# Five places for the low halves of the weights, a negated half made from the high half, and a convolution without padding

## The chip, the core and the metric

The kernel runs on one core of one Trainium2 chip. TensorE does the matmuls; VectorE, ScalarE and GpSimd prepare operands and take results out of PSUM; the queues of SyncE (SP) and GpSimd (POOL) issue the transfers from HBM. The metric is the device time of one launch in microseconds, as the median of the runs shown.

## The reference

Two layers, each of three sublayers with a residual: a SwiGLU feed-forward block (FFN), a mixing sublayer, and another FFN. Sequence 512, model width 1024, all in float32.

```
for l in range(DEPTH):
    h = swiglu_ffn(rmsnorm(x, ffn1_pre_g[l]), ffn1_w_gu[l], ffn1_w_down[l])
    x = x + 0.5 * rmsnorm(h, ffn1_post_g[l])
    h = mixing_sublayer(rmsnorm(x, mix_pre_g[l]), w_in[l], ...)
    x = x + rmsnorm(h, mix_post_g[l])
    h = swiglu_ffn(rmsnorm(x, ffn2_pre_g[l]), ffn2_w_gu[l], ffn2_w_down[l])
    x = x + 0.5 * rmsnorm(h, ffn2_post_g[l])
...
def mixing_sublayer(h, ...):
    z = h @ w_in
    uv, pz, qz, kz, vz, qi, ki, wi, cz, gz = jnp.split(z, ...)
    branches = (gmlp_mixer(uv, ...), pool_mixer(pz, ...), sparse_attention(qz, kz, vz, qi, ki, wi, rel_bias),
                conv_mixer(cz, ...))
    gates = jax.nn.sigmoid(gz.reshape(B, S, N_BRANCH, D_MODEL))
    y = gates[:, :, 0] * (branches[0] @ w_branch[0])
    for n in range(1, N_BRANCH):
        y = y + gates[:, :, n] * (branches[n] @ w_branch[n])
    return y @ w_out
...
def conv_mixer(ab, dw, db, ln_g, ln_b):
    a, gt = jnp.split(ab, 2, axis=-1)
    h = a * jax.nn.sigmoid(gt)
    h = lax.conv_general_dilated(h, dw[:, None, :], window_strides=(1,), padding=[(CONV_K - 1, 0)], ...) + db
    return jax.nn.silu(layernorm(h, ln_g, ln_b))
```

The convolution is causal, depthwise, of 31 taps over 256 channels.

## The kernel before

Everything lies transposed: features on the 128 partitions, the 512 positions along the row. A product of float32 matrices is made of three products in the faster `float32r` type: each operand is split into a high half (rounded) and a low half (the rest), and high x high, high x low and low x high are summed in PSUM. For one tile of 128 output features and 1024 input features that is 24 matmuls of 512 columns (`mm3s`, line 253). They go in this order: for the first seven blocks of inputs high and low half of the weights in turn (so the low half is first needed by the second matmul), then the seven with the low half of x, then the last block's three.

The weights come as tiles of 128x1024 (512 KB) through `weights` (lines 180 to 203). SP loads the tile into `raw` (two places in SBUF). ScalarE makes the high half `wH` from it (line 197; four places). The low half `wL` (four places) is made in one of two ways:

- in the FFNs, VectorE subtracts: `wL = raw - wH` (line 202);
- for tiles called with `far=True`, ScalarE writes the negated high half into `wL` as a rounded, negated copy of `raw` (line 199), and POOL issues a second transfer of the same weights from HBM that is added to it on arrival (line 200). All of the mixing sublayer's columns of `w_in` after the first six, its `w_branch` and the first half of its `w_out` tiles go this way, and the tiles that open a sublayer.

A place of `wH` or `wL` comes free when TensorE has read the tile in it for the last time. The last reader of a low half is the matmul before the last one of its tile, that of a high half the last.

The mixing sublayer (`Mix.rest`) works through 50 columns of `w_in`; the last 32 are the gates (`Mix.gates`). A gate column takes its 24 matmuls, VectorE scales the result (`th`, line 756), ScalarE takes its tanh (line 757), then six matmuls with a `w_branch` tile follow, and VectorE multiplies the two (line 766, or 764 on a branch's first visit). One `w_branch` tile serves four columns and holds its place of `wH` and `wL` all that time, so the columns turn over in the other three. Beside it generators run that are stepped between columns (`pump`): attention with its top-k, the pooling, the gated MLP and the convolution (`conv`), which on VectorE is one multiply-add over 512 positions for each tap and each half of the channels (line 865). The padded input of the convolution (`hp`, tag "cv") has 30 zeros in front, written by POOL (line 699).

The order of the instructions on each engine is fixed when the program is built, by a scheduler that places what its own estimate holds ready. On an engine nothing overtakes: an instruction that waits holds all behind it. Temporaries ("t") have twelve places; in the trace names carry no buffer numbers.

Of the kernel before, what the change touches and what calls it, by code (L numbers as in the profile page):

```python
# [11 lines left out]
F32 = mybir.dt.float32  # L12
F32R = mybir.dt.float32r
I32 = mybir.dt.int32
AF = mybir.ActivationFunctionType
ALU = mybir.AluOpType
AX = mybir.AxisListType

P = 128
N = 512  # L20
# [9 lines left out]
CONV_K = 31  # L30
# [12 lines left out]
V_PS, V_CB, V_LG, V_LB, V_DW = 48, 50, 52, 54, 56  # L43
# [6 lines left out]
class Builder:  # L50
# [17 lines left out]
        return self.sb.tile(shape, dt, name=f"{tag}_{self.n}", tag=tag, bufs=bufs)  # L68

    def tmp(self, dt=F32, w=N):  # L70
        return self.t([P, w], dt, "t", 12)

    def ring(self, dt=F32R):
        return self.t([P, N], dt, "h", 20)
# [105 lines left out]
    def weights(self, src, n, ring=False, raw=None, far=False):  # L180

        nc = self.nc
        raw = raw or self.t([P, 1024], F32, "raw", 2)
        nc.sync.dma_start(raw[:, :n], src)
        if ring:
            hs, ls = [], []
            for i in range(2):
                h, lo = self.ring(), self.ring()
                r = raw[:, i * N:(i + 1) * N]
                nc.scalar.activation(h, r, AF.Copy)  # L190
                nc.gpsimd.tensor_tensor(lo, r, h.bitcast(F32), op=ALU.subtract)
                hs.append(h)
                ls.append(lo)
            return hs, ls
        h = self.t([P, 1024], F32R, "wH", 4)
        lo = self.t([P, 1024], F32R, "wL", 4)
        self.pin(nc.scalar.activation(h[:, :n], raw[:, :n], AF.Copy))  # L197
        if far:
            self.pin(nc.scalar.activation(lo[:, :n], raw[:, :n], AF.Copy, scale=-1.0))  # L199
            nc.gpsimd.dma_start(lo[:, :n], src, accum_op=ALU.add)  # L200
            return h, lo
        self.pin(nc.vector.tensor_tensor(lo[:, :n], raw[:, :n], h.bitcast(F32)[:, :n], op=ALU.subtract))  # L202
        return h, lo
# [362 lines left out]
class Mix:  # L566
# [84 lines left out]
    def rest(self):  # L651
        b, nc, l = self.b, self.b.nc, self.l

        z = self.norm(T_KI)
        kih, kil = b.ring(), b.ring()
        nc.scalar.activation(kih[0:96], z[0:96], AF.Copy)
        nc.scalar.activation(kih[96:128], z[0:32], AF.Copy)
        khf = kih.bitcast(F32)
        nc.vector.tensor_tensor(kil[0:96], z[0:96], khf[0:96], op=ALU.subtract)
        nc.vector.tensor_tensor(kil[96:128], z[0:32], khf[0:32], op=ALU.subtract)  # L660
        pw = b.pt("at")
        for c in range(4):
            nc.tensor.transpose(pw[:, c * 32:(c + 1) * 32], z[96:128, c * P:(c + 1) * P], b.ident[96:128, 96:128])
        self.wi = b.t([P, 4, 4], F32, "wi", 1)
        nc.scalar.activation(self.wi, pw[:, :P].rearrange("p (c k) -> p c k", k=32)[:, :, 0:4], AF.Copy, scale=0.5)
        self.ki = (kih, kil)
        self.qi = b.split(self.norm(T_QI))
        self.q = [b.split(self.norm(T_Q + j, scale=0.125)) for j in range(2)]
        self.k = [b.split(self.norm(T_K + j)) for j in range(2)]
        sc, zv = {}, []  # L670
        for j, i in enumerate((3, 2)):
            sc[i] = self.scores(i)
            zv.append(self.norm(T_V + j))
        sc[1] = self.scores(1)
        zp = [self.norm(T_P)]
        self.vv = []
        for cp in range(2):
            pv = b.pt("at")
            for c in range(2):
                for j in range(2):  # L680
                    nc.tensor.transpose(pv[:, c * 256 + j * P:c * 256 + (j + 1) * P],
                                        zv[j][:, (2 * cp + c) * P:(2 * cp + c + 1) * P], b.ident)
            h, lo = b.t([P, N], F32R, "av", 4), b.t([P, N], F32R, "av", 4)
            b.split(pv, h, lo)
            self.vv.append((h, lo))
        self.busy = False
        attn = [self.attention(i, sc.get(i)) for i in range(4)]
        self.b2 = [(b.ring(), b.ring()) for _ in range(2)]
        b.bg += attn
        pool = [self.pool(zp + [self.norm(T_P + 1)])]  # L690
        b.bg[:0] = pool

        self.hpad = []
        for j in range(2):
            zg = self.norm(T_CZ + 2 + j)
            nc.scalar.activation(zg, zg, AF.Tanh, scale=0.5)
            za = self.norm(T_CZ + j, scale=0.5)
            hp = b.t([P, N + CONV_K - 1], F32, "cv", 2)
            nc.gpsimd.memset(hp[:, 0:CONV_K - 1], 0.0)
            nc.vector.scalar_tensor_tensor(hp[:, CONV_K - 1:], zg, 1.0, za, op0=ALU.add, op1=ALU.mult)  # L700
            self.hpad.append(hp)
        conv = [self.conv()]
        b.bg[:0] = conv
        zv = [self.norm(T_UV + 2 + j) for j in range(2)]
        u = []
        for j in range(2):
            z = self.norm(T_UV + j)
            nc.scalar.activation(z, z, AF.Gelu_apprx_tanh)
            u.append(z)
        gmlp = [self.gmlp(zv, u)]  # L710
        b.bg[:0] = gmlp
        self.y = [None] * KD
        self.ym = []
        b.finish(pool)
        self.gates(1, self.b1, 5000)
        b.finish(gmlp)
        self.gates(0, self.b0, 5000)
        b.finish(conv)
        self.gates(3, self.b3, 5000)
        b.finish(attn)  # L720
        self.gates(2, self.b2, 5000)
        self.o = [None] * KD
        self.sq = b.tmp()
        for d0 in range(0, KD - TAIL, 2):
            ds = range(d0, d0 + 2)
            w = [b.weights(b.a["w_out"][l, d], 1024, far=True) for d in ds]
            p = [b.cyc() for d in ds]
            b.gemms(p, w, self.ym)
            for i, d in enumerate(ds):
                self.o[d] = b.t([P, N], F32, "y", 8)  # L730
                nc.scalar.activation(self.o[d], p[i], AF.Copy)
                b.sq_add(self.sq, self.o[d], FULL, d == 0)
# [121 lines left out]
    def conv(self):  # L854
        b, nc, l = self.b, self.b.nc, self.l
        acc = []
        ca = b.t([P, 2 * N], F32, "ca", 1)
        for j in range(2):
            a = ca[:, j * N:(j + 1) * N]
            hp = self.hpad[j]  # L860
            dw = lambda t: b.v(l, V_DW + t * 2 + j)
            nc.vector.tensor_scalar(a, hp[:, 0:N], dw(0), b.v(l, V_CB + j), op0=ALU.mult, op1=ALU.add)
            yield 450
            for t in range(1, CONV_K):
                nc.vector.scalar_tensor_tensor(a, hp[:, t:t + N], dw(t), a, op0=ALU.mult, op1=ALU.add)  # L865
                if t % 2 == 0:
                    yield 1360
            acc.append(a)
        both = b.tmp()
        nc.gpsimd.tensor_tensor(both, acc[0], acc[1], op=ALU.add)  # L870
        yield 0, 1
        ps = b.compact([both], FULL)
        mu = b.s8(4)
        nc.vector.tensor_scalar(mu, ps, 1.0 / C, None, op0=ALU.mult)
        dg = b.diag(mu, FULL, 1.0)
        yield 500, 1
        pb = b.spread(dg, FULL)
        sq = []
        for j in range(2):
            nc.vector.tensor_tensor(acc[j], acc[j], pb, op=ALU.subtract)  # L880
            q = b.tmp()
            nc.scalar.activation(q, acc[j], AF.Square)
            sq.append(q)
        nc.gpsimd.tensor_tensor(sq[0], sq[0], sq[1], op=ALU.add)
        yield 1200, 1
        ps = b.compact([sq[0]], FULL)
        ms, r = b.s8(4), b.s8(4)
        nc.vector.tensor_scalar(ms, ps, 1.0 / C, EPS, op0=ALU.mult, op1=ALU.add)
        b.rsqrt(r, ms)
        dg = b.diag(r, FULL)  # L890
        yield 1500, 1
        pb = b.spread(dg, FULL)
        self.b3 = []
        for j in range(2):
            nc.vector.tensor_tensor(acc[j], acc[j], pb, op=ALU.mult)
            nc.vector.tensor_scalar(acc[j], acc[j], self.ln2[:, j:j + 1], self.ln2[:, 2 + j:3 + j],
                                    op0=ALU.mult, op1=ALU.add)
            th = b.tmp()
            nc.scalar.activation(th, acc[j], AF.Tanh)
            nc.vector.scalar_tensor_tensor(th, th, 1.0, acc[j], op0=ALU.add, op1=ALU.mult)  # L900
            self.b3.append(b.split(th))
            yield 2300
# [165 lines left out]
```

## Time and profile before

| | |
|---|---|
| median of three runs | 2319.39 us (2319.12 to 2322.17) |
| the profiled execution | 2320.38 us, of it 2318.7 us span |
| TensorE busy | 2279.7 us, 98% of the span |
| VectorE busy | 1192.4 us, 51% |
| ScalarE busy | 924.5 us, 40% |
| GpSimd busy | 249.8 us, 11% |
| mean granted TensorE clock | 0.996 |

The mixing sublayers lie at about 385 to 760 us and 1530 to 1905 us, the FFNs around them. TensorE is at work nearly all the time, so what a change is worth is what it takes from, or adds to, the few stretches in which TensorE stands still. Of its 39 us of idle time some 9 lie ahead of the first products and some 14 behind the last; the rest is in the mixing sublayers and at the seams.

### The profile page before, as it was taken

The numbers are of one execution on the slowest core, as the hardware profiler recorded it, in microseconds if no ns is written. First come the engines' busy times: TensorE is split into PE (matmuls) and PEld (weight loads), VectorE is DVE, ScalarE is ACT, GpSimd is POOL, SyncE is SP. The second block draws the span as 40 slices with busy tenths as digits, with TensorE's granted clock in tenths as the row PEclk, the third lists the DMA queues.
The fourth block names the chain that finished last, engine by engine and source line by source line (L and its number), as shares of the span: only waits on it lengthen the run. The fifth ranks groups of instructions, "written<-read, shape, count | busy, mean of one in ns | idle before, by whom it ended". The sixth has DMA issues, their size and how long they took to land.

```text
span 2318.7 us, 28250 instructions
## 1 busy us (share of the span) xinstructions
PE 2279.7 (98%) x11158; PEld 1907.0 (82%) x11158; DVE 1192.4 (51%) x2144; ACT 924.5 (40%) x1350; POOL 249.8 (11%) x291
## 2 busy tenths in 40 slices
PE   8999999999999999999999999999999999999997
PEld 6888889777788988888888888897778889888886
DVE  5333337799433552434473334478984337424345
ACT  4232225564554532222342222355545545322221
POOL 0000002211331200000100000023123212000001
PEclk9999999999999999999999999999999999999998
DMA  5333323867778433233343333247677774332322
GB/s 170 92 107 92 108 90 94 187 148 169 176 167 182 119 100 98 93 101 95 94 113 95 110 92 100 91 122 162 148 180 178 174 164 110 100 93 93 105 88 68
DMA packets 82557, 282.27 MB, mean 122 GB/s; under 512 B 9428, under 2 KB 13176, under 8 KB 82424
## 3 DMA queue, kind: packets, MB, share of 16 engines
q1 hardware_dynamic: 64136, 213.87, 29.2%
q0 software_dynamic: 18288, 66.59, 16.7%
q8 instruction: 87, 1.43, 0.2%
q14 instruction: 46, 0.38, 0.0%
HBM read 278.32 MB, written 2.10 MB: 121 GB/s over the span
## 4 chain that ended last, share of the span: by engine, by line
PE 88%; DVE 6%; DMA 2%; ACT 2%; issue 2%; POOL 0%; SPq 0%; POOLq 0%; DVEq 0%; ACTq 0%
PE mm L253 51%; PE at L253 31%; DVE ca L865 2%; PE mm L287 2%; PE at L287 2%; DMA wL<-in_w_in_dram 1%; DMA raw<-in_w_in_dram 1%; ACT wH L197 1%; PE st L330 1%; PE st L314 1%; ACT wL L199 1%; DMA wL<-in_ffn_w_gu_dram 0%; ACT xH L408 0%; DVE sc L935 0%; DVE m L934 0%
## 5 line engine op out<-in xcount | busy, mean ns | idle before, releaser
L197 ACT ACTIVATE wH<-raw 128x1024 fp32r<-128x1024 f32 (+1 forms) x394 | 407.4, 1037 | 831.4 <-issue 562.6
L253 PE MATMUL mm<-xH,wH 128*128 128x512 f32 x1344 | 530.8, 396 | 1.5 <-DVE t L756 1.5
L253 PE MATMUL mm<-xH,wL 128*128 128x512 f32 x1344 | 525.7, 392 | 5.3 <-DMA wL<-in_w_in_dram 5.3
L202 DVE TENSOR_TENSOR wL<-raw,wH 128x1024 fp32r<-128x1024 f32 (+1 forms) x272 | 324.2, 1194 | 248.5 <-ACT wH L197 248.4
L253 PE MATMUL mm<-h,wH 128*128 128x512 f32 (+1 forms) x1496 | 409.2, 354 | 0.3 <-DVE t L756 0.3
L253 PE MATMUL mm<-xL,wH 128*128 128x512 f32 x1344 | 358.9, 389 | 0.0
L253 PEld LDWEIGHTS mm<-xH,wL 128*128 128x128 f32 x1344 | 253.6, 189 | 60.2 <-DMA wL<-in_w_in_dram 7.6
L253 PEld LDWEIGHTS mm<-xH,wH 128*128 128x128 f32 x1344 | 253.5, 189 | 58.5 <-issue 4.2
L253 PEld LDWEIGHTS mm<-h,wH 128*128 128x128 f32 x1496 | 263.8, 188 | 41.7 <-DVE t L756 0.5
L253 PEld LDWEIGHTS mm<-xL,wH 128*128 128x128 f32 x1344 | 252.3, 188 | 52.4
L253 PE MATMUL at<-xH,wH 128*128 128x512 f32 x704 | 277.8, 396 | 8.1 <-ACT xH L223 7.3
L253 PE MATMUL at<-xH,wL 128*128 128x512 f32 x704 | 274.5, 392 | 0.0
L253 PE MATMUL mm<-h,wL 128*128 128x512 f32 (+1 forms) x748 | 252.4, 352 | 0.0
L253 PE MATMUL at<-h,wH 128*128 128x512 f32 (+1 forms) x776 | 219.6, 366 | 0.0
L199 ACT ACTIVATE wL<-raw 128x1024 fp32r<-128x1024 f32 x122 | 128.6, 1054 | 179.5 <-PE mm L253 151.0
L253 PE MATMUL at<-xL,wH 128*128 128x512 f32 x704 | 187.8, 389 | 0.0
L253 PEld LDWEIGHTS at<-xH,wH 128*128 128x128 f32 x704 | 133.1, 189 | 38.6 <-ACT xH L223 7.7
L253 PEld LDWEIGHTS at<-h,wH 128*128 128x128 f32 x776 | 140.4, 188 | 24.6
L253 PEld LDWEIGHTS at<-xH,wL 128*128 128x128 f32 x704 | 133.1, 189 | 29.5 <-issue 1.4
L253 PEld LDWEIGHTS mm<-h,wL 128*128 128x128 f32 x748 | 140.4, 188 | 20.3
L253 PEld LDWEIGHTS at<-xL,wH 128*128 128x128 f32 x704 | 132.2, 188 | 27.5
L253 PE MATMUL at<-h,wL 128*128 128x512 f32 (+1 forms) x388 | 136.5, 366 | 0.0
(212 smaller groups left out, 2260.7 us busy)
## 6 DMA issues: line engine op xcount, KB each, us to landing
raw<-in_ffn_w_gu_dram SPq DMA_DIRECT2D x173, 512.0 KB, 3.6
raw<-in_w_in_dram SPq DMA_DIRECT2D x98, 512.0 KB, 6.5
wL<-in_w_in_dram POOLq DMA_DIRECT2D x94, 512.0 KB, 7.1
raw<-in_ffn_w_down_dram SPq DMA_DIRECT2D x64, 448.0 KB, 3.3
raw<-in_ffn_w_down_dram SPq DMA_DIRECT2D x32, 512.0 KB, 3.5
raw<-in_w_branch_dram SPq DMA_DIRECT2D x16, 512.0 KB, 5.3
wL<-in_w_branch_dram POOLq DMA_DIRECT2D x16, 512.0 KB, 7.0
raw<-in_w_out_dram SPq DMA_DIRECT2D x16, 512.0 KB, 6.3
```

Source lines behind the costliest of these rows:

```text
L197: self.pin(nc.scalar.activation(h[:, :n], raw[:, :n], AF.Copy))
L199: self.pin(nc.scalar.activation(lo[:, :n], raw[:, :n], AF.Copy, scale=-1.0))
L202: self.pin(nc.vector.tensor_tensor(lo[:, :n], raw[:, :n], h.bitcast(F32)[:, :n], op=ALU.subtract))
L253: self.nc.tensor.matmul(out, w[a], m[b], start=(first and i == 0), stop=(last and i == 3 * n - 1))
L287: self.nc.tensor.matmul(out, w[a], m[b], start=(count[j] == 1), stop=(count[j] == 3 * KD))
L314: self.nc.tensor.matmul(ps[:, c - c0:c - c0 + 1], s[:, c * P:(c + 1) * P], self.ones[:, 0:1], start=(i == 0), stop=(i == len(tiles) - 1))
L330: self.nc.tensor.matmul(ps[:, s], self.ones, dg[:, s], start=True, stop=True)
L865: nc.vector.scalar_tensor_tensor(a, hp[:, t:t + N], dw(t), a, op0=ALU.mult, op1=ALU.add)
```

## The change

Four things are changed.

1. `wL` has five places instead of four; `wH` keeps four. The room comes from the temporaries, which go from twelve places to eleven.
2. The negated half of a `far` tile is read from `wH` instead of `raw` (line 199): ScalarE now has to write `wH` first.
3. The convolution's input has no padding: `hp` is 512 wide, its two zero-fills on POOL are gone.
4. The taps run from the last to the first, and tap `s` covers the 512 - s positions that it reaches.

```diff
     def tmp(self, dt=F32, w=N):
-        return self.t([P, w], dt, "t", 12)
+        return self.t([P, w], dt, "t", 11)
...
         h = self.t([P, 1024], F32R, "wH", 4)
-        lo = self.t([P, 1024], F32R, "wL", 4)
+        lo = self.t([P, 1024], F32R, "wL", 5)
         self.pin(nc.scalar.activation(h[:, :n], raw[:, :n], AF.Copy))
         if far:
-            self.pin(nc.scalar.activation(lo[:, :n], raw[:, :n], AF.Copy, scale=-1.0))
+            self.pin(nc.scalar.activation(lo[:, :n], h.bitcast(F32)[:, :n], AF.Copy, scale=-1.0))
             nc.gpsimd.dma_start(lo[:, :n], src, accum_op=ALU.add)
             return h, lo
...
-            hp = b.t([P, N + CONV_K - 1], F32, "cv", 2)
-            nc.gpsimd.memset(hp[:, 0:CONV_K - 1], 0.0)
-            nc.vector.scalar_tensor_tensor(hp[:, CONV_K - 1:], zg, 1.0, za, op0=ALU.add, op1=ALU.mult)
+            hp = b.t([P, N], F32, "cv", 2)
+            nc.vector.scalar_tensor_tensor(hp, zg, 1.0, za, op0=ALU.add, op1=ALU.mult)
...
-            nc.vector.tensor_scalar(a, hp[:, 0:N], dw(0), b.v(l, V_CB + j), op0=ALU.mult, op1=ALU.add)
+            nc.vector.tensor_scalar(a, hp, dw(CONV_K - 1), b.v(l, V_CB + j), op0=ALU.mult, op1=ALU.add)
             yield 450
-            for t in range(1, CONV_K):
-                nc.vector.scalar_tensor_tensor(a, hp[:, t:t + N], dw(t), a, op0=ALU.mult, op1=ALU.add)
-                if t % 2 == 0:
+            for s in range(1, CONV_K):
+                nc.vector.scalar_tensor_tensor(a[:, s:], hp[:, :N - s], dw(CONV_K - 1 - s), a[:, s:],
+                                               op0=ALU.mult, op1=ALU.add)
+                if s % 2 == 0:
                     yield 1360
```

The order on the engines moves with it. On ScalarE, among the last gate columns of layer 0 (`wL_5836` belongs to the tile first multiplied at 718 us in the trace; `t` with line 757 is the tanh of the column that has just been finished, `h` with line 223 the split of a finished sum), the rows stand so before:

```order
L199 ACTIVATE wL_5836<-raw_5833 128x1024
L197 ACTIVATE wH_5835<-raw_5833 128x1024
L757 ACTIVATE t_5762<-t_5762 128x512
L223 ACTIVATE h_5774<-y_4150 128x512
L199 ACTIVATE wL_5884<-raw_5881 128x1024
L197 ACTIVATE wH_5883<-raw_5881 128x1024
L757 ACTIVATE t_5810<-t_5810 128x512
```

and so after the change:

```order
L197 ACTIVATE wH_5833<-raw_5831 128x1024
L756 ACTIVATE t_5760<-t_5760 128x512
L199 ACTIVATE wL_5834<-wH_5833 128x1024
L223 ACTIVATE h_5772<-y_4148 128x512
L197 ACTIVATE wH_5881<-raw_5879 128x1024
L756 ACTIVATE t_5808<-t_5808 128x512
L199 ACTIVATE wL_5882<-wH_5881 128x1024
```

The negated half stood first in each round and now stands third, behind the high half and the tanh.

On ScalarE, in the first round of gates of layer 0 (`wL_4253` is first multiplied at 530 us; `s` and line 957 to 959 are the softmax of the attention, line 220 the splits of other branches), before:

```order
L959 ACTIVATE t_4097<-t_4097,s_789_4101 128x256
L199 ACTIVATE wL_4253<-raw_4250 128x1024
L197 ACTIVATE wH_4252<-raw_4250 128x1024
L757 ACTIVATE t_4140<-t_4140 128x512
L199 ACTIVATE wL_4316<-raw_4313 128x1024
L220 ACTIVATE y_4173<-t_4053 128x512
L757 ACTIVATE t_4209<-t_4209 128x512
L197 ACTIVATE wH_4315<-raw_4313 128x1024
```

and after:

```order
L959 ACTIVATE t_4095<-t_4095,s_789_4099 128x256
L197 ACTIVATE wH_4250<-raw_4248 128x1024
L199 ACTIVATE wL_4251<-wH_4250 128x1024
L756 ACTIVATE t_4138<-t_4138 128x512
L197 ACTIVATE wH_4313<-raw_4311 128x1024
L220 ACTIVATE y_4171<-t_4051 128x512
L756 ACTIVATE t_4207<-t_4207 128x512
L220 ACTIVATE t_4227<-at_4222 128x512
L199 ACTIVATE wL_4314<-wH_4313 128x1024
```

Here the first negated half moves behind its high half, with nothing else between; the second one moves from the fifth row to the ninth, behind a tanh and two splits.

On VectorE, at the attention's split that TensorE waits for at 482 us (`t_3756`, line 221), before:

```order
L865 SCALAR_TENSOR_TENSOR ca_3767<-cv_3716,vec,ca_3767 128x512
L865 SCALAR_TENSOR_TENSOR ca_3767<-cv_3568,vec,ca_3767 128x512
L865 SCALAR_TENSOR_TENSOR ca_3767<-cv_3716,vec,ca_3767 128x512
L865 SCALAR_TENSOR_TENSOR ca_3767<-cv_3568,vec,ca_3767 128x512
L221 TENSOR_TENSOR t_3756<-at_3752,t_3755 128x256
```

and after:

```order
L864 SCALAR_TENSOR_TENSOR ca_3765<-cv_3715,vec,ca_3765 128x511
L864 SCALAR_TENSOR_TENSOR ca_3765<-cv_3568,vec,ca_3765 128x504
L864 SCALAR_TENSOR_TENSOR ca_3765<-cv_3715,vec,ca_3765 128x510
L864 SCALAR_TENSOR_TENSOR ca_3765<-cv_3568,vec,ca_3765 128x503
L864 SCALAR_TENSOR_TENSOR ca_3765<-cv_3715,vec,ca_3765 128x509
L221 TENSOR_TENSOR t_3754<-at_3750,t_3753 128x256
```

The same taps stand ahead of the split; they are a little shorter.

## Rows read from the trace of the kernel before

**Rows 1.** Stretches of the two mixing sublayers: us, busy by engine, clock, DMA share, GB/s.

```profile
400.00:760.00 360.00, 352.60 (x1648) 286.09 (x1648) 232.77 (x501) 196.78 (x299) 89.78 (x104) 0.99 0.74 168
...
1540.00:1900.00 360.00, 353.37 (x1699) 288.49 (x1698) 239.81 (x512) 199.90 (x305) 91.11 (x103) 1.00 0.73 167
```

**Rows 2.** Timeline of TensorE, matmuls that waited: start, us, [idle before <-releaser].

```profile
482.53 0.41 PE L253 MATMUL at<-t,av 128*128 128x256 f32 x1 [2.37 <-DVE t L221]
...
530.16 0.50 PE L253 MATMUL mm<-xH,wL 128*128 128x512 f32 x1 [3.09 <-DMA wL<-in_w_in_dram]
...
570.96 0.50 PE L253 MATMUL mm<-xH,wL 128*128 128x512 f32 x1 [0.54 <-DMA wL<-in_w_in_dram]
...
1673.21 0.50 PE L253 MATMUL mm<-xH,wL 128*128 128x512 f32 x1 [0.23 <-DMA wL<-in_w_in_dram]
...
1682.08 0.55 PE L969 MATMUL at<-ident,t 128*128 128x128 f32 x3 [1.87 <-ACT t L959]
...
1684.81 0.50 PE L253 MATMUL mm<-xH,wL 128*128 128x512 f32 x1 [0.57 <-DMA wL<-in_w_in_dram]
...
1695.33 0.50 PE L253 MATMUL mm<-xH,wH 128*128 128x512 f32 x1 [1.52 <-DVE t L756]
```

**Rows 3.** Waits, all engines: who waited for whom: us in total, times, longest.

```profile
ACT wL L199 <- PE mm L253: 151.0, 55, 5.2
...
PE mm L253 <- DMA wL<-in_w_in_dram: 5.3, 5, 3.1
```

**Rows 4.** Timeline of ScalarE in one round of the last gates.

```profile
710.05 1.06 ACT L199 ACTIVATE wL<-raw 128x1024 fp32r<-128x1024 f32 x1 [2.24 <-PE mm L253]
711.02 1.04 ACT L197 ACTIVATE wH<-raw 128x1024 fp32r<-128x1024 f32 x1
711.96 0.61 ACT L757 ACTIVATE t<-t 128x512 f32<-128x512 f32 x1
```

**Rows 5.** POOL's part of that round: its timeline, then the tile's time to landing.

```profile
711.41 0.86 POOL L200 DMA_DIRECT2D wL<-in_w_in_dram  x1 [6.04 <-ACT wL L199]
...
DMA to landing us min/median/max: 6.9/6.9/6.9
```

**Rows 6.** Timeline of TensorE, first uses of the tile: high half, low half.

```profile
718.35 0.40 PE L253 MATMUL mm<-xH,wH 128*128 128x512 f32 x1
718.58 0.39 PE L253 MATMUL mm<-xH,wL 128*128 128x512 f32 x1
```

**Rows 7.** Timeline of VectorE: the scaling ahead of a tanh, in three rounds.

```profile
562.55 0.69 DVE L756 TENSOR_TENSOR t<-mm,rb__553_3031 128x512 f32<-128x512 f32 x1
...
710.28 0.69 DVE L756 TENSOR_TENSOR t<-mm,rb__553_3031 128x512 f32<-128x512 f32 x1 [1.74 <-PE mm L253]
...
1711.11 0.68 DVE L756 TENSOR_TENSOR t<-mm,rb__2307_12256 128x512 f32<-128x512 f32 x1
```

**Rows 8.** Timeline of ScalarE at 561 us.

```profile
561.72 1.06 ACT L199 ACTIVATE wL<-raw 128x1024 fp32r<-128x1024 f32 x1 [1.84 <-PE mm L253]
```

**Rows 9.** A tile of w_out: negation, time to landing, first uses of two tiles' low halves.

```profile
737.57 1.06 ACT L199 ACTIVATE wL<-raw 128x1024 fp32r<-128x1024 f32 x1 [2.24 <-PE mm L253]
...
DMA to landing us min/median/max: 6.8/6.8/6.8
...
746.33 0.62 PE L253 MATMUL at<-h,wL 128*128 128x512 f32 x2
```

**Rows 10.** Two rounds of layer 1: ScalarE's negations, TensorE's first use of the first.

```profile
1701.31 1.04 ACT L199 ACTIVATE wL<-raw 128x1024 fp32r<-128x1024 f32 x1
...
1707.74 1.06 ACT L199 ACTIVATE wL<-raw 128x1024 fp32r<-128x1024 f32 x1 [2.23 <-PE mm L253]
...
1709.45 0.50 PE L253 MATMUL mm<-xH,wL 128*128 128x512 f32 x1
```

**Rows 11.** The taps of the convolution, line 865: times, ns min/median/max.

```profile
L865 DVE SCALAR_TENSOR_TENSOR ca<-cv,vec,ca x120: 723/743/2241, 467.1 to 1704.8; 128x512 f32<-128x512 f32 x120
```

**Rows 12.** The stretch around a long wait; the last three figures are clock, DMA, GB/s.

```profile
527.00:535.00 8.00, 4.91 (x15) 3.86 (x15) 8.00 (x19) 5.22 (x7) 0.07 (x2) 0.79 0.91 225
```

## The prediction

> **What bounds the kernel now.** I read the stretches first. In the two windows that hold the mixing sublayers TensorE is busy 352.6 of 360 us and 353.4 of 360 [rows 1], and the 14 us missing there are nearly all that a change inside these sublayers can win back. So the question is which TensorE waits there are, and what ends each. The timeline of TensorE gives them [rows 2]: some end with the arrival of a low half of weights (530, 571, 1673, 1685 us), some with VectorE or a softmax (482, 1682, 1695 us). All waits for low halves of `w_in` sum to 5.3 us, five times [rows 3]. Then I followed one round of the last gate columns, to see how near the others are to waiting. The negation starts at 710.05, the moment TensorE frees the place [rows 4]; the transfer is issued at 711.41 and lands 6.9 us later [rows 5], at 718.3; TensorE first reads the tile at 718.58 [rows 6]. So 0.3 us are to spare. Such rounds do not show in any list of waits, yet anything that makes the negation later than 0.3 us stops TensorE there.
>
> **The fifth place.** ScalarE's negation has waited 151 us in total for TensorE to free a place of `wL` [rows 3]; with five places that wait goes. But the negation now reads `wH`, which keeps four places, and a high half's place comes free one matmul after the low half's: 0.23 us by two starts in a row [rows 6]. The wait moves one instruction ahead, to the high half. Gain 0, and 0.23 us are lost.
>
> The Trainium skill, Perfetto Trace Analysis, section Optimization Strategy, says that gaps repeating on the engine that should be saturated can mean that there is no SBUF for the next tile, buffer count among the reasons. It speaks for a fifth place; by it the 5.3 us would go, and it is the first rival below. The rows fit its diagnosis, but the place that is short after the change is one that the change does not add.
>
> **The order on ScalarE, the main term.** In a round of the last gates the order was negation, high half, tanh; it becomes high half, tanh, negation. The high half takes 0.97 us from start to start [rows 4]. The tanh needs VectorE's scaling, which ends at 710.28 + 0.69 = 710.97 [rows 7], before the high half would be done; so it runs at once and takes 0.5 to 0.6 us [rows 4]. The negation comes 0.23 + 0.97 + 0.55 = 1.7 us later, and with it everything up to the landing. Of that 0.3 us are covered: TensorE waits 1.4 us. The next column is as tight, but its place is freed before this wait and its use comes after, so the wait covers it: counted once for such a pair. The six places where this decides, by their rows:
>
> - 530 us: TensorE already waits 3.09 us [rows 2]; the order there puts only the high half ahead, so +1.0 [rows 4].
> - 571 us: it already waits 0.54 us [rows 2], so nothing is covered. The negation was at 561.72 [rows 8]; VectorE's scaling ends at 562.55 + 0.69 = 563.24 [rows 7], the tanh at about 563.9, so the negation is 2.1 us late: +2.1.
> - last gates of layer 0: +1.4, as above.
> - `w_out`, layer 0: negated at 737.57, issued 1.36 us later as in [rows 4, 5], landed after 6.8 us at 745.7; its first use is the second of two matmuls from 746.33 [rows 9], so about 0.8 us are to spare, and 1.7 - 0.8 = +0.9.
> - the last gates and `w_out` of layer 1 are built the same: +1.4 and +0.9.
> - layer 1, 1709 and 1716 us: at 1701.31 the negation gets the high half ahead of it. Its landing, after 1.36 and about 6.9 us, is 1709.6, and TensorE reads it at 1709.45 [rows 10], so nothing is to spare: +1.0. The next one was at 1707.74 [rows 10] and will stand behind a tanh whose scaling VectorE finished only at 1711.79 [rows 7]; that would be 4.7 us late. From it go the 1.0 us for which TensorE was just held and what VectorE has gained by then. Bounds 0.5 (VectorE in time: 1.7 - 1.0 - 0.2) and 3.5 us; I take 2.0.
>
> The stretch of 1673 to 1696 us in layer 1 has two waits for low halves and two for VectorE's work [rows 2]. The low halves come later by 1.0 and about 2 us. But where TensorE is held, VectorE's work goes on, and the two waits it caused, 1.87 and 1.52 us [rows 2], shrink by as much. Between 0 (all absorbed) and 3.0 us (nothing) I take 1.5.
>
> Sum: layer 0, 1.0 + 2.1 + 1.4 + 0.9 = 5.4; layer 1, 1.5 + 1.0 + 2.0 + 1.4 + 0.9 = 6.8; together 12.2 us. The remaining rounds of the gates have more than 1.4 us to spare and add tenths at most.
>
> **The raw tile** is now read by one ScalarE instruction instead of two, so SP's next load starts about 1 us sooner. No TensorE wait in the list ends with a raw tile [rows 2]: 0.
>
> **The convolution.** The 30 shortened taps leave out 1 + 2 + ... + 30 = 465 positions for each half of the channels. At 743 ns for 512 positions [rows 11] that is at most 465 x 1.45 ns = 0.7 us for each of two halves, 1.35 us of VectorE a layer. TensorE's wait at 482 us (2.37 us [rows 2]) stands behind taps, but the same number as before, and the few shortened by then save under 0.1 us. Gain 0 to 1.3 us a layer; taken as 0, since it is counted in the two bounds above. The two zero-fills were POOL's alone, of 30 columns: 0.
>
> **One temporary fewer.** No row shows a wait for a temporary's place. Bounds: 0, and the longest wait for a softmax row, 1.87 us [rows 2]. Taken as 0, since the order on VectorE is nearly the same. In the FFNs the low half was always made from the high half, so neither the fifth place nor the order moves anything there: 0.
>
> **The clock.** Around the 3.09 us wait the mean granted clock was 0.79 over 8 us [rows 12]: 3.4 us at the lower of the two levels, 1.2 GHz, which costs 1.7 us of work. That wait stays. Of the new waits, those at 571 and 1716 us (2.7 and 2 us) are nearest to it in length. I leave the clock out of the sum and put it into the range.
>
> **The rivals.**
>
> *The fifth place pays.* If the negation were in fact ready sooner (the high half's place free well before the low half's), the waits for low halves would go: 5.3 us [rows 3], and 1.7 us of clock, 2312.4 us. It ends on the other side, and it decides at the place: if `wH` is free when the low half's fifth place is. Against it: the high half's last reader follows the low half's in every tile, and both have held four. Chance 0.08.
>
> *The delay is mostly covered.* Where VectorE lets the tanh run late in all rounds or TensorE's other waits absorb it, only 530, 571 and the last gates count, about +5: 2324.5. For it: VectorE's waits in both layers [rows 2]. Against it: the last gates of both layers have no such wait. Chance 0.20.
>
> *All hidden.* Transfers land sooner since ScalarE starts them further apart, and nothing moves: 2319. Against it: a delay of 1.7 us stands against a spare of 0.3 us in the last gates. Chance 0.05.
>
> *The clock falls too.* The waits at 571, 1685 and 1716 us each bring the lower level, at 1.7 us: 2331.5 + 5 = 2336.6, and more if what I called absorbed is not. Chance 0.12.
>
> **How the numbers follow.** The profiled execution took 2320.38 us, 1.0 above the median of the runs. 2320.4 + 12.2 = 2332.6; against the median, 2331.6, rounded to 2331.5. This forecast (2326 to 2335) has chance 0.55. The range goes from the covered case with its lower edge (2321) to the clock case (2338); outside lie the first rival, part of the hidden case, and the far end of the clock case, some 0.16. A difference of 0.2% (4.6 us) is about what a measurement of this kernel tells from none. Slower by more: the forecast, the clock case and six tenths of the covered case, 0.55 + 0.12 + 0.12 = 0.79. Within 0.2%: the hidden case and the rest of the covered one, 0.13. Faster: 0.08.
>
> **What the profile after would show.** Right: ScalarE's wait for TensorE stands at line 197, and line 199 waits for it no more; TensorE waits 1 to 2 us for a low half near the ends of both layers' gates and 0.5 to 1 us at `w_out`; the total of its waits for `wL` is near 17 us instead of 5.3; the FFN stretches keep their time. Wrong: TensorE's busy share of the mixing sublayers stays or rises, the last gates show no wait, or a new wait stands at a temporary or at SP's loads.

## The result, and the profile after

| | before | after |
|---|---|---|
| median of the runs, us | 2319.55 | 2338.55 |
| profiled execution: its time, us | 2320.38 | 2340.61 |
| its span, us | 2318.7 | 2338.9 |
| TensorE busy, us | 2279.7 | 2289.6 |
| TensorE idle (span less busy), us | 39.0 | 49.3 |
| mean granted clock of TensorE | 0.996 | 0.993 |

The changed kernel is slower. The medians lie 19.0 us apart; over all runs the ratio is 1.0076, with a 95% interval of 1.0064 to 1.0087, some 18 us. The forecast was 2331.5, in a range of 2321 to 2338: the median lies 0.55 us above its upper edge, while 1.0076 times the 2319.39 us that the forecast started from is 2337.0, inside it. The profiled execution lost 20.2 us: TensorE is idle for 10.3 us more and busy for 9.9 us more, at the same number of matmuls.

The page of the changed kernel, its busy times:

```profile
PE 2289.6 (98%) x11158; PEld 1911.6 (82%) x11158; DVE 1196.1 (51%) x2144; ACT 927.4 (40%) x1350; POOL 246.6 (11%) x287
```

The table of its waits, which answers to [rows 3] (us in total, times, longest):

```profile
PE mm L253 <- DMA wL<-in_w_in_dram: 19.0, 11, 3.9
...
ACT wH L197 <- PE mm L253: 307.8, 89, 8.9
```

and the second of these rows in the kernel before:

```profile
ACT wH L197 <- PE mm L253: 94.3, 24, 8.8
```

TensorE now waits 19.0 us for low halves of `w_in`, not 5.3. ScalarE's wait for TensorE at line 197 has grown from 94.3 to 307.8 us; at line 199, where it was 151.0 us, there is none. The seven longest of TensorE's eleven waits for low halves, from its timeline, as [rows 2]:

```profile
506.38 0.70 PE L253 MATMUL mm<-xH,wL 128*128 128x512 f32 x1 [3.89 <-DMA wL<-in_w_in_dram]
...
573.70 0.50 PE L253 MATMUL mm<-xH,wL 128*128 128x512 f32 x1 [2.14 <-DMA wL<-in_w_in_dram]
...
732.58 0.50 PE L253 MATMUL mm<-xH,wL 128*128 128x512 f32 x1 [1.44 <-DMA wL<-in_w_in_dram]
...
1663.01 0.50 PE L253 MATMUL mm<-xH,wL 128*128 128x512 f32 x1 [2.82 <-DMA wL<-in_w_in_dram]
...
1729.97 0.50 PE L253 MATMUL mm<-xH,wL 128*128 128x512 f32 x1 [3.05 <-DMA wL<-in_w_in_dram]
...
1761.38 0.50 PE L253 MATMUL mm<-xH,wL 128*128 128x512 f32 x1 [1.06 <-DMA wL<-in_w_in_dram]
...
1888.16 0.50 PE L253 MATMUL mm<-xH,wL 128*128 128x512 f32 x1 [2.18 <-DMA wL<-in_w_in_dram]
```

The round of [rows 4 to 6] in the changed kernel: ScalarE, then the issue on POOL, then TensorE's first use of the low half.

```profile
715.60 1.06 ACT L197 ACTIVATE wH<-raw 128x1024 fp32r<-128x1024 f32 x1 [3.19 <-PE mm L253]
716.56 0.61 ACT L756 ACTIVATE t<-t 128x512 f32<-128x512 f32 x1
717.08 1.04 ACT L199 ACTIVATE wL<-wH 128x1024 fp32r<-128x1024 f32 x1
...
718.41 0.86 POOL L200 DMA_DIRECT2D wL<-in_w_in_dram  x1 [6.04 <-ACT wL L199]
...
724.01 0.50 PE L253 MATMUL mm<-xH,wL 128*128 128x512 f32 x1
```

High half, tanh, negation: the negation begins 1.48 us after the high half, which is 0.96 + 0.52 from the three starts. That is the order, and with the 0.23 us of the place the delay, that the prediction gave for this round.

One stretch ahead of the gates holds the longest wait. ScalarE there, after:

```profile
490.12 1.06 ACT L197 ACTIVATE wH<-raw 128x1024 fp32r<-128x1024 f32 x1
...
494.89 0.63 ACT L707 ACTIVATE t<-t 128x512 f32<-128x512 f32 x1 [2.41 <-DVE t L646]
...
498.87 0.51 ACT L959 ACTIVATE t<-t,s 128x256 f32<-128x256 f32 x1 [0.77 <-DVE s L958]
499.29 1.05 ACT L199 ACTIVATE wL<-wH 128x1024 fp32r<-128x1024 f32 x1
```

and before, where the negation came first:

```profile
489.78 1.06 ACT L199 ACTIVATE wL<-raw 128x1024 fp32r<-128x1024 f32 x1 [0.98 <-PE mm L253]
```

Between the high half and the negation made from it now stand the GELU of the gated MLP (line 707), which waits for VectorE, and three steps of a softmax, 9.2 us from start to start. The transfer lands at 506.3 and TensorE waits 3.89 us. The same piece of the order in layer 1, there 8.9 us from start to start, gives the 2.82 us at 1663.

The clock: 8 us windows around the places where it fell (the last three figures are clock, DMA share, GB/s). Before, in the middle of the kernel, only those around 482 and 530 us read 0.79, the second in [rows 12], the first here:

```profile
479.00:487.00 8.00, 5.63 (x20) 0.79 1.01 246
```

After:

```profile
503.00:511.00 8.00, 4.62 (x13) 0.79 0.92 219
571.00:579.00 8.00, 5.86 (x19) 0.79 1.04 256
1571.00:1579.00 8.00, 7.69 (x28) 0.79 0.96 219
1636.00:1644.00 8.00, 5.87 (x20) 0.79 1.00 239
1660.00:1668.00 8.00, 5.18 (x16) 0.79 0.92 215
1885.00:1893.00 8.00, 5.82 (x19) 0.79 1.04 256
```

Six falls to the lower level (1.2 GHz) instead of two. At the 1.7 us that the prediction worked out for one, four more are 6.8 of TensorE's 9.9 us of longer busy time.

### The profile page after: what moved, and what is told of

Same layout as the page of the kernel before. It is cut to its first block, busy times and chain, and to the rows that moved or that the text cites. A ratio compares the mean times of both kernels' runs of the same rounds, so it can differ in the third digit from the quotient of the medians.

```text
span 2338.9 us, 28346 instructions
## 1 busy us (share of the span) xinstructions
PE 2289.6 (98%) x11158; PEld 1911.6 (82%) x11158; DVE 1196.1 (51%) x2144; ACT 927.4 (40%) x1350; POOL 246.6 (11%) x287
## 4 chain that ended last, share of the span: by engine, by line
PE 79%; DVE 7%; issue 7%; DMA 3%; ACT 2%; POOL 1%; POOLq 0%; SPq 0%; DVEq 0%; ACTq 0%
PE mm L253 42%; PE at L253 31%; DMA wL<-in_w_in_dram 2%; PE mm L287 2%; PE at L287 2%; DVE sc L935 1%; DVE m L934 1%; DVE ca L864 1%; POOL wL L200 1%; PE st L330 1%; ACT wH L197 1%; PE st L314 1%; ACT wL L199 0%; ACT xH L408 0%; DVE t L400 0%
## 5 line engine op out<-in xcount | busy, mean ns | idle before, releaser
L199 ACT ACTIVATE wL<-wH 128x1024 fp32r<-128x1024 f32 x127 | 133.2, 1049 | 1.2
```

The lines of the kernel that those rows point to most:

```text
L199: self.pin(nc.scalar.activation(lo[:, :n], h.bitcast(F32)[:, :n], AF.Copy, scale=-1.0))
```

## The experiments

All ratios are against runs of the kernel before on the same chip, with 95% intervals. Theory 1 was the prediction's: the loss comes from the source of the negation, because the place that is short is that of the high half.

**Which part carries the loss.** First the change without its second part:

```
-            self.pin(nc.scalar.activation(lo[:, :n], h.bitcast(F32)[:, :n], AF.Copy, scale=-1.0))
+            self.pin(nc.scalar.activation(lo[:, :n], raw[:, :n], AF.Copy, scale=-1.0))
```

> The changed kernel with one line put back: the negated half is again made from raw (five places for low halves, four for high halves, eleven temporaries and the unpadded convolution stay). Theory 1, the negation's source: it no longer stands behind the high half and the tanh, so the 20 us go and the fifth place is even used; TensorE's waits for low halves fall below the 5.3 us of the kernel before, 2312 to 2318 us. Theory 2, the loss sits in the other parts (one temporary fewer, the convolution, a changed order on VectorE): 2330 to 2338 us, and the waits for low halves stay near 19 us.

Measured: 2444.38 us, ratio 1.0526 (1.0507 to 1.0546). Both theories fell for this run: it is 106 us slower than the full change. Its timeline of ScalarE, and SyncE's queue in the same stretch (three loads from 609.48 on):

```profile
607.45 1.06 ACT L199 ACTIVATE wL<-raw 128x1024 fp32r<-128x1024 f32 x1 [7.58 <-DMA raw<-in_w_in_dram]
608.41 1.04 ACT L197 ACTIVATE wH<-raw 128x1024 fp32r<-128x1024 f32 x1
...
616.21 1.06 ACT L199 ACTIVATE wL<-raw 128x1024 fp32r<-128x1024 f32 x1 [6.24 <-DMA raw<-in_w_in_dram]
...
609.48 17.73 SPq L184 DMA_DIRECT2D raw<-in_w_in_dram  x3
```

The time from issue to landing of the raw tiles there:

```profile
DMA to landing us min/median/max: 6.2/6.4/6.5
```

and the negation's wait for raw tiles in the whole run:

```profile
ACT wL L199 <- DMA raw<-in_w_in_dram: 298.0, 69, 8.0
```

The high half at 608.41 belongs to the tile before the one negated at 607.45. With a free low place the negation runs one tile ahead of the high half, so a tile stays in `raw` from its negation to its high half, some 10 us, and both raw places are taken. The next load goes out only after the high half (609.48), lands 6.4 us later, and ScalarE stands for it until 616.21 with tanh and softmax behind it. So the second part of the change is also what makes a fifth low place bearable with two `raw` places.

Then the second part alone, on the kernel before:

```
-            self.pin(nc.scalar.activation(lo[:, :n], raw[:, :n], AF.Copy, scale=-1.0))
+            self.pin(nc.scalar.activation(lo[:, :n], h.bitcast(F32)[:, :n], AF.Copy, scale=-1.0))
```

> The kernel before with only the source of the negation changed to the high half (four and four places, twelve temporaries, padded convolution). Theory 1: the source alone carries the loss, 2333 to 2340 us, ScalarE's wait for TensorE moves from the negation to the high half, and TensorE's waits for low halves come to 15 to 20 us. Theory 2: 2318 to 2324 us.

Measured: 2334.19 us, ratio 1.0049 (1.0030 to 1.0069); the medians lie 13.4 us apart. From its waits:

```profile
PE mm L253 <- DMA wL<-in_w_in_dram: 18.1, 12, 3.5
...
ACT wH L197 <- PE mm L253: 307.1, 91, 8.9
```

Both waits are within a microsecond of those of the full change. Theory 1 holds: the source of the negation carries most of the loss without any of the other parts.

**Which place is short.** In the changed kernel, the fifth place goes to the high halves:

```
-        h = self.t([P, 1024], F32R, "wH", 4)
-        lo = self.t([P, 1024], F32R, "wL", 5)
+        h = self.t([P, 1024], F32R, "wH", 5)
+        lo = self.t([P, 1024], F32R, "wL", 4)
```

> The changed kernel with the fifth place given to the high halves instead of the low ones (wH 5, wL 4); the negation still reads the high half. Theory 1a, the place that is short is that of the high half: the high half is written a tile early, the negation waits only for its own place as in the kernel before, 2314 to 2322 us, ScalarE's wait for TensorE is back at the negation. Theory 1b, it is the order alone (the negation stands behind the tanh whichever place is free): 2333 to 2340 us.

Measured: 2317.25 us, ratio 0.9984 (0.9974 to 0.9995). From its waits:

```profile
PE mm L253 <- DMA wL<-in_w_in_dram: 3.4, 3, 1.4
```

Its timeline of ScalarE in the round that answers to [rows 4]:

```profile
707.93 1.06 ACT L199 ACTIVATE wL<-wH 128x1024 fp32r<-128x1024 f32 x1 [2.24 <-PE mm L253]
708.90 1.05 ACT L197 ACTIVATE wH<-raw 128x1024 fp32r<-128x1024 f32 x1
709.85 0.61 ACT L756 ACTIVATE t<-t 128x512 f32<-128x512 f32 x1
```

The negation still reads the high half, but that half was written a tile earlier; it waits 2.24 us for its own place, to the hundredth as in [rows 4], and the next high half and the tanh stand behind it. With the right place the loss is gone and a little more. The place and the order move together here: with a high half's place free early, the scheduler also puts the negation ahead of the tanh again, and no run holds one of the two still while the other moves. The Trainium skill, Perfetto Trace Analysis, section Optimization Strategy, says that repeated gaps can point to the buffer count; here they did, but it was a fifth place for the high halves, and not the one for the low halves, that filled them (3.4 us of waits against 19.0 us).

The low halves back at four, all else as changed:

```
-        lo = self.t([P, 1024], F32R, "wL", 5)
+        lo = self.t([P, 1024], F32R, "wL", 4)
```

> The changed kernel with the low halves back at four places; everything else of the change stays (negation from the high half, eleven temporaries, unpadded convolution). The order of instructions on every engine is the same as in the changed kernel. Theory 1, the fifth place is never used, since the negation waits for the high half, whose place comes free last: the same time as the changed kernel, 2335 to 2341 us, TensorE's waits for low halves 17 to 21 us. Rival, the fifth place gives back part of the loss: 2342 us or more without it.

Measured: 2339.43 us, ratio 1.0084 (1.0071 to 1.0098), with this wait:

```profile
PE mm L253 <- DMA wL<-in_w_in_dram: 18.4, 14, 4.5
```

The fifth low place does nothing in the changed kernel: without it the order is the same and so is the time.

Five places for both:

```
-        return self.t([P, w], dt, "t", 11)
+        return self.t([P, w], dt, "t", 9)
-        h = self.t([P, 1024], F32R, "wH", 4)
+        h = self.t([P, 1024], F32R, "wH", 5)
```

> Five places for both halves, paid with two more temporaries (nine instead of eleven); the negation reads the high half. Theory 1a: neither half waits for a place when its turn comes, the transfers go out up to a tile earlier, TensorE's waits for low halves nearly vanish, 2308 to 2316 us. Against it: nine temporaries delay the softmax and the taps on VectorE, waits for VectorE's temporaries appear, 2320 to 2340 us.

Measured: 2319.99 us, ratio 0.9992 (0.9982 to 1.0002): no difference from before. The page has no wait ahead of the matmuls that read low halves (the last figure):

```profile
L253 PE MATMUL mm<-xH,wL 128*128 128x512 f32 x1344 | 525.5, 392 | 0.0
```

The waits for low halves are gone, and nothing is gained: TensorE's waits for VectorE's scaling grew from 1.8 to 3.4 us and for VectorE's low halves (line 221) from 4.7 to 6.8 us. Which of the nine temporaries and the new order did that was not told apart.

**The small parts.** The unpadded convolution alone on the kernel before (the lines of `conv` as in the change), and then with eleven temporaries too:

```
-            hp = b.t([P, N + CONV_K - 1], F32, "cv", 2)
+            hp = b.t([P, N], F32, "cv", 2)
...
-        return self.t([P, w], dt, "t", 12)
+        return self.t([P, w], dt, "t", 11)
```

> The kernel before with the unpadded convolution alone (places four and four, twelve temporaries, negation from raw). Theory of the prediction: 0, with 1.35 us of VectorE less a layer: 2317 to 2322 us. Rival: the part of the loss that the negation alone did not show (19.0 - 13.4 = about 5.6 us) comes from the convolution's new order on VectorE: 2323 to 2328 us.

> The unpadded convolution and eleven temporaries on the kernel before (negation from raw, places four and four). Against the run with the convolution alone it shows the temporary. Prediction: 0, 2317 to 2322 us. Rival: the missing temporary makes a wait on VectorE or ScalarE and costs 2 to 6 us, 2323 to 2328 us.

Measured: 2322.03 us, ratio 1.0010 (1.0001 to 1.0019), and 2322.27 us, ratio 1.0009 (1.0000 to 1.0018). The convolution by itself costs about 2 us, hardly clear of nothing, and the temporary adds nothing that these runs can tell. In the first of the two TensorE's waits for low halves are 6.3 us instead of 5.3 and those for VectorE's scaling 3.0 instead of 1.8, although VectorE is busy for 1.1 us less.

Between the medians the parts alone sum to 13.4 + 2.2 = 15.6 of 19.0 us. The rest, 3.4 us, lies within the interval of the negation's part (7 to 16 us) and was not traced to a part of the change. It is hardly waiting: in the profiled execution with the negation alone, the fastest of its four, TensorE is idle for 47.3 us against 49.3 in the full change, but busy for 2282.8 us against 2289.6, at a mean granted clock of 0.995 against 0.993.

**POOL.** In 26 of the 60 rounds of the gates and `w_out` after them (each issue's start less its negation's), the issue comes 0.8 us or so later than elsewhere, since a gate's addition now stands ahead of it on POOL. The additions go to VectorE:

```
-                e = nc.vector if n == 2 else nc.gpsimd
+                e = nc.vector
```

> The changed kernel with the gates' additions to y (28 of 512 columns on GpSimd, 1.28 us each) moved to VectorE, so that no addition stands ahead of a transfer's issue on GpSimd. In the changed kernel 26 of 60 issues come 0.8 us or more later than the 1.35 us after the negation's start that the others show. If that is a part of the loss, TensorE's waits for low halves fall from 19 to 8 to 13 us, and the time to 2328 to 2334 us. If VectorE's longer rounds (0.65 us more for each column) hold the tanh and so the negation, nothing is won: 2337 us or more.

Measured: 2339.89 us, ratio 1.0086 (1.0073 to 1.0100); nothing is won. The time from issue to landing, 576 to 770 us, of this run:

```profile
DMA to landing us min/median/max: 5.4/6.6/8.5
```

of the changed kernel:

```profile
DMA to landing us min/median/max: 5.2/5.7/7.9
```

and of the kernel before:

```profile
DMA to landing us min/median/max: 5.2/7.0/9.0
```

The transfers go out sooner but take 0.9 us longer, so the waits for low halves stay (19.9 us). The time is in the second range that was expected, but not for the reason given there: the negation still begins 1.48 us after its high half in most rounds, and ScalarE's tanh waits 6.7 us for the scaling, not longer than the 7.3 us without the move. A raw load starts about a microsecond after each high half; the later the low half's transfer, the more of that load is over, which would explain the three rows. The Trainium skill, DMA: Bandwidth & Descriptors, Rules for kernel authors, says that transfers issued from SyncE, ScalarE or GpSimd all run on the same DMA engines and interleave; the three rows fit that, but none of them shows it alone.

**Better versions, and what the source costs.** The kernel before with five high places and the padded convolution:

```
-        return self.t([P, w], dt, "t", 12)
+        return self.t([P, w], dt, "t", 11)
-        h = self.t([P, 1024], F32R, "wH", 4)
+        h = self.t([P, 1024], F32R, "wH", 5)
-            self.pin(nc.scalar.activation(lo[:, :n], raw[:, :n], AF.Copy, scale=-1.0))
+            self.pin(nc.scalar.activation(lo[:, :n], h.bitcast(F32)[:, :n], AF.Copy, scale=-1.0))
```

> The kernel before with five places for high halves, eleven temporaries and the negation from the high half; low halves at four, the convolution padded as before. If the convolution's new form costs the 2 us seen when it stood alone, this is the better version: 2314 to 2317 us, TensorE's waits for low halves at most 5 us. If that cost belonged to the order around it, it is the same as with the unpadded convolution: 2317 to 2320 us.

Measured: 2317.45 us, ratio 0.9991 (0.9982 to 1.0000). It is no better than with the unpadded form (2317.25 us, 0.9974 to 0.9995), so the 2 us of the convolution do not show here. With the waits named above that points to the order around it rather than to its work; it was not traced further.

The changed kernel with five high and four low places and the negation from `raw`:

```
-        h = self.t([P, 1024], F32R, "wH", 4)
-        lo = self.t([P, 1024], F32R, "wL", 5)
+        h = self.t([P, 1024], F32R, "wH", 5)
+        lo = self.t([P, 1024], F32R, "wL", 4)
-            self.pin(nc.scalar.activation(lo[:, :n], h.bitcast(F32)[:, :n], AF.Copy, scale=-1.0))
+            self.pin(nc.scalar.activation(lo[:, :n], raw[:, :n], AF.Copy, scale=-1.0))
```

> Five places for high halves, four for low ones, eleven temporaries, the unpadded convolution, and the negation from raw. Theory: with the high half's place free a tile early the source of the negation no longer matters, and the negation waits only for its own place: 2315 to 2323 us. Rival: the negation holds raw until its place is free, SyncE's next load starts later than in the kernel before, and ScalarE stands before a raw tile that has not landed: over 2335 us.

Measured: 2331.94 us, ratio 1.0053 (1.0035 to 1.0070), between the two expectations. From its waits:

```profile
ACT wH L197 <- DMA raw<-in_w_in_dram: 35.0, 25, 4.9
ACT wH L197 <- DMA raw<-in_w_branch_dram: 21.7, 6, 5.4
ACT wH L197 <- DMA raw<-in_w_out_dram: 8.9, 6, 4.3
```

and from its timeline, ScalarE at one such wait and the matmul of TensorE held by the softmax behind it:

```profile
1785.98 1.06 ACT L197 ACTIVATE wH<-raw 128x1024 fp32r<-128x1024 f32 x1 [3.90 <-DMA raw<-in_w_in_dram]
...
1788.79 0.33 PE L969 MATMUL at<-ident,t 128*128 128x128 f32 x1 [2.32 <-ACT t L959]
```

Now the high half runs ahead and the negation holds `raw`. At the high half ScalarE waits 65.6 us for raw tiles of the mixing sublayers; in the kernel before it was 27.8 us at the negation and 6.5 at the high half. In the place shown the softmax stands behind such a wait and TensorE waits 2.32 us for it. The rival's mechanism is there, at a smaller size than it was put at.

Then two ways out of the first run's trouble, both from its kernel (five low places, negation from `raw`) and both with nine temporaries. Five places for the high halves too:

```
-        h = self.t([P, 1024], F32R, "wH", 4)
+        h = self.t([P, 1024], F32R, "wH", 5)
```

> Five places for both halves, nine temporaries, negation from raw. The run with five low and four high places and the negation from raw took 2444 us: ScalarE stood 298 us before negations whose raw tile had not landed, since the raw place is held by the tile before, whose high half waits for its place. Theory a, it was the mismatch of the places: with both at five the copy of the high half follows at once and frees raw, 2316 to 2330 us. Theory b, with any free low place the negation is put ahead of work that is ready, and ScalarE stands before the load in any case: over 2380 us.

or a third raw place (in all five lines that name it):

```
-        raw = raw or self.t([P, 1024], F32, "raw", 2)
+        raw = raw or self.t([P, 1024], F32, "raw", 3)
```

> Five low and four high places, the negation from raw, and a third raw place paid with two temporaries (nine). Theory a, two raw places are what makes ScalarE stand: with a third the next load is already there when the negation's turn comes, ScalarE's waits for raw fall from 298 to under 100 us and the time to 2315 to 2345 us. Theory b, as above: over 2380 us.

Measured: 2326.71 us, ratio 1.0026 (1.0013 to 1.0039), and 2316.45 us, ratio 0.9984 (0.9973 to 0.9996). Of the last, ScalarE's wait:

```profile
ACT wL L199 <- DMA raw<-in_w_in_dram: 12.2, 7, 4.1
```

From 298.0 us to 12.2 with one more raw place: theory a holds, the two held raw places made ScalarE stand in the first run. With five places for both halves the same wait is 15.0 us, so there theory a holds too, at 2326.71 us. The version with a third raw place and the one with five high places have the lowest ratios of all, 0.16% or some 3 to 4 us below the kernel before; both intervals end just short of none.

## Why the prediction was right, and where its numbers fell short

**The mechanism was right.** The wait moved to line 197; the negation stands behind high half and tanh; the source alone gives the waits (2334.19 us), the fifth low place nothing (2339.43 us without it), and a fifth high place takes them away (2317.25 us). The total of TensorE's waits for low halves was put near 17 us and is 19.0.

**The sum of waits was about right, its places less so.** It put 12.2 us of new waits; TensorE's idle time grew by 10.3. That the two are so near is in part luck: the 571 us place, 1716 us and the last gates of both layers gave 8.2 us where 6.9 were put, the other places that it named gave nothing together (-0.4) where 5.3 were put, and rounds that it put at tenths gave 3.5.

| place | put at, us | measured, us |
|---|---|---|
| 530 us | +1.0 | 3.89 at 506 and 0.07 at 532, instead of 3.09: +0.9 |
| 571 us | +2.1 | 2.14 instead of 0.54: +1.6 |
| 627 us | not named | none instead of 0.86: -0.9 |
| last gates, layer 0 | +1.4 | none at 724, 1.44 one column on: +1.4 |
| `w_out`, both layers | +0.9 each | none |
| 1673 to 1696 us | +1.5 | 2.82 at 1663 instead of 0.23 + 1.87 + 0.57 + 1.52: -1.4 |
| 1709 us | +1.0 | 0.13 |
| 1716 us | +2.0 | 3.05 (bounds 0.5 and 3.5) |
| last gates, layer 1 | +1.4 | 2.18 |
| other rounds | tenths | 1.06 at 1761, four more of 0.26 to 0.87 |

Three steps of this sum failed. The step "the remaining rounds have more than 1.4 us to spare" took 1.7 us for the delay everywhere; ahead of the gates it is 9.2 us, because the order puts GELU and softmax between the two halves, and the waits at 506 and 1663 come from there. In the sum they took the place of later ones (530, and the two for VectorE in layer 1) as much as they added. One row of the kernel before spoke against that step already, one of the five waits that [rows 3] counts, which [rows 2] and the prediction lack:

```profile
627.18 0.50 PE L253 MATMUL mm<-xH,wL 128*128 128x512 f32 x1 [0.86 <-DMA wL<-in_w_in_dram]
```

The second is the landing, carried over at 6.9 us, and with it the raw tile, costed at 0. The raw load now starts ahead of the low half's transfer in most rounds from 576 to 770 us: at 716.68 ahead of the issue at 718.41, which landed after 5.6 us; the `w_out` tile issued at 747.83 took 5.7 us, and the tile issued at 1713.66 took 6.1. That gain covers `w_out`, most of the 1.0 us at 1709, and the first of the last gates. The next tile was issued at 725.30, ahead of the load at 725.98; it took 7.2 us, and TensorE waited 1.44 us for it. The third is the stretch of 1673 to 1696, where the waits for VectorE were to shrink; they vanished.

**What was missing is the clock.** The rival "the clock falls too" had the size (three falls, 5 us) and a chance of 0.12; in the profiled execution there were four more falls, 6.8 us. 2320.4 + 10.3 of idle + 6.8 is 2337.5; 3.1 us of longer busy time are left, which no row here assigns. Against the sum of 2332.6 this is the whole difference of 8.0 us: fewer waits than put (-1.9), the clock (+6.8), and the unassigned 3.1. The six executions of the changed kernel say the same: the two with a mean clock of 0.995 took 2332.47 and 2335.69 us, the four with 0.993 took 2338.29 to 2340.61. So the forecast, which had no clock in it, is near the time of the execution that lost least by it, and the range came near the median only by its clock case. The clock should have been a term of the sum, with waits of 2 to 4 us growing in number.

**The other points.** The temporary: 0, as put (2322.27 us with it, 2322.03 without). The convolution: put at 0 to -1.3 us a layer, measured +2 alone and nothing with five high places; its work is as small as put (VectorE is busy for 1.1 us less in both layers together), its effect on the order was not considered. The rival "the fifth place pays" fell where the prediction said it would, at the high half's place; it is true of the other buffer.

## What to carry to other kernels

Before adding a place to a buffer, ask which of the buffers that a step reads and writes comes free last: a step that is made to read another buffer inherits that buffer's wait, and the place belongs there. A source that is read twice is held from the first reading to the second; when a free place lets the first run ahead, the load behind it stops, and an engine that works in order stands in front of it. Sum the waits, but give each wait of some microseconds its chance of a slower clock as well.

## What was not expected of the hardware

The clock does not follow the waits one by one. Around the 3.05 us wait at 1730 it stayed at the upper level (2.4 GHz), while at 1574 it fell after nothing longer than 0.31 us in the 14 us before. After:

```profile
1727.00:1735.00 8.00, 5.03 (x22) 1.00 1.06 257
```

and in the run with the low halves back at four places, which has the same order of instructions, in the same two windows of the program:

```profile
1727.00:1735.00 8.00, 5.69 (x18) 0.79 1.06 256
...
571.00:579.00 8.00, 5.92 (x27) 1.00 1.01 259
```

There it fell at 1730, and not in the window of 571 to 579, where it had fallen in the changed kernel. So which waits bring a fall differs between runs of one order. Their number does too: it is six in both of these executions, but the mean clock of the changed kernel's executions goes from 0.993 to 0.995. A sum can take a mean number of falls, and the range has to hold their spread.
